# The second score product of the B heads, from a contraction of 64 rows to one of 128

## The chip, the cores and the metric

The kernel runs on one core of one Trainium2 chip. The metric is the device time of one execution in microseconds (us), smaller is better. TensorE is named PE in the profile (its weight loads PEld), VectorE DVE, ScalarE ACT, GpSimd POOL, SyncE SP.

## The reference, cut to what matters

The model is a decoder trunk of two layers on one sequence of 512 tokens with 1024 features. Each layer is an attention part and a gated MLP. The attention part has 16 heads in three groups that share one input and one output projection: A (4 heads, differential attention), B (6 heads, a mixture of dilated windows) and C (6 heads, a learned forget bias). The change touches B alone:

```python
qb = apply_rope(heads(qb, B_HEADS), cos_b, sin_b)          # 6 heads of 64 features
kb = apply_rope(heads(kb, B_HEADS), cos_b, sin_b)
ob = dilated_mixture_attention(qb, kb, heads(vb, B_HEADS))
# inside, for each of three dilated windows:
s = jnp.einsum('bgnqd,bgnkd->bgnqk', qb, kk).astype(jnp.float32) * (hd ** -0.5)
```

All of it is float32. The score of a query and a key is the product of two vectors of 64 features. The kernel forms the mixture of the three windows as one softmax with a mask that carries the logarithm of how many windows hold a pair, so that each B head needs one score matrix, causal, of 512 by 512.

## The kernel before, in words

**Splitting into high and low.** PE multiplies numbers of the type fp32r, which keeps fewer bits than float32. So each operand is split in two: the high part is what fp32r keeps (a copy on ACT), and the low part is the rest (a subtraction on DVE). A product then takes several matmuls: high by high, low by high, high by low. In the projections that is the helper `mm3` (lines 265 to 267), three matmuls of 512 columns for each tile of 128 features.

**Layout of q and k.** Heads are worked on in pairs; a pair fills 128 rows (partitions), 64 for each head, and `H0`, `H1` are the two halves. `stack_gen` (from line 427) builds the operands of a pair from the projection after rope. For q (`side == 0`) there is one tile for each head, with the high part in the head's own half and the low part in the other half. For k (`side == 1`) of the B heads there is one tile for each head with the high part in both halves (the first copy at line 436, the second at line 447), and a third tile, shared by both heads, with the low part of each head in its own half (line 433 is the subtraction). C heads have four tiles on each side; their second tiles hold 64 rows plus 4 rows of the forget bias.

**Score products.** `emit_S` (from line 620) makes the scores of one block: 128 queries against n keys, n being 128, 256, 384 or 512 for the four blocks of a head. Line 630 contracts all 128 rows: (high and low of q) by (high of k twice). For B heads line 632 then adds 64 rows: high of q by low of k, taken from the half `r` of the head. For C heads line 634 adds the 68 rows of their second tiles instead. A heads take one matmul of 96 rows (line 640).

**Order of the work.** In each layer eight pairs are worked on in the order B0 B1 A0 C0 A1 C1 B2 C2. Each pair has eight blocks (two heads of four). For a block come the scores (PE), the mask with its row maximum (line 653, DVE), the exponential (line 666, ACT), then two blocks later the transposes (line 694, PE), the split of the transposed weights (lines 713 on ACT and 718 on DVE) and the product with v (lines 740 and 741, PE). In between `fill` puts matmuls of the projections that later pairs need: the q and k chunks of the next pair (`qk_chunk`) and the v projections (`v_half`), and for the last pair the output projection. Post-processing (rope, `stack_gen`, the splits, the end of a head) stands in generators on a list; `tick` takes one step of each after every few matmuls. The tile framework orders each engine's instructions from this and sets the semaphores.

**Buffers.** All q and k operand tiles come from one pool of 14 tiles (`QKB`) of 128 by 512. A pair of B heads takes 5 of them, a pair of A or C heads 8.

**Around it.** While layer 0's attention runs, a stream of modulation weights is multiplied on POOL (line 221) and summed on ACT (line 224), for later use. The weights of the projections are loaded by DMA in order, and split on ACT (line 174) and DVE (line 186).

Of the kernel before, what the change touches and what calls it, by code (L numbers as in the profile page):

```python
# [8 lines left out]
F32 = mybir.dt.float32  # L9
F32R = mybir.dt.float32r  # L10
AF = mybir.ActivationFunctionType
# [19 lines left out]
def kernel(  # L31
# [27 lines left out]
    V, A, T, G = nc.vector, nc.scalar, nc.tensor, nc.gpsimd  # L59
# [15 lines left out]
    def tmp(name, tag):  # L75
        if tag == "rp":
            return rpp[0].tile([128, SEQ], F32, tag=tag, name=name, bufs=4)
        return tp.tile([128, SEQ], F32, tag=tag, name=name, bufs=4)
# [37 lines left out]
    for l in range(DEPTH):  # L116
# [16 lines left out]
        for m in range(KC):  # L133
            for b in range(0, FC, 8):
                n = min(8, FC - b)
# [117 lines left out]
    def split_gen(src, hi, lo):  # L253
        A.activation(out=hi, in_=src, func=AF.Copy)
        yield
        V.tensor_tensor(out=lo, in0=src, in1=hi.bitcast(F32), op=ALU.subtract)
        yield
# [23 lines left out]
    H0, H1 = slice(0, 64), slice(64, 128)  # L281
# [97 lines left out]
    def layer_attn(l, ap, mods, st, rt0):  # L379
        h = st.h  # L380
# [48 lines left out]
        def stack_gen(src, side, res, pair=None):  # L429
            R = (H0, H1)  # L430

            def sub(out, h):
                V.tensor_tensor(out=out, in0=src[R[h]], in1=res[h][R[h]].bitcast(F32), op=ALU.subtract)

            for h in range(2):
                A.activation(out=res[h][R[h]], in_=src[R[h]], func=AF.Copy)
                yield
                if side == 0:
                    sub(res[h][R[1 - h]], h)
                elif pair is None:  # L440
                    sub(res[2][R[h]], h)
                else:
                    sub(res[2 + h][H0], h)
                yield
                dup = res[h][R[1 - h]] if side == 1 else res[2 + h][H0] if pair is not None else None
                if dup is not None:
                    A.activation(out=dup, in_=src[R[h]], func=AF.Copy)
                yield
            if pair is not None:
                while not aug:  # L450
                    yield
                for h in range(2):
                    c = 24 * side + 4 * (2 * (pair - 5) + h)
                    nc.sync.dma_start(out=res[2 + h][64:68, :].bitcast(F32), in_=aug[0][c:c + 4, :].bitcast(F32))
                yield

        def qk_post(idx, side, ps, kind):
            n = 2 + side if kind == "B" else 4
            res = [ap.tile([128, SEQ], F32R, tag="qk", name="qk", bufs=QKB) for _ in range(n)]
            qks[idx, side] = res  # L460
            if kind == "C":
                yield from stack_gen(ps, side, res, ORDER[idx][1])
                qkdone.add((idx, side))
                return
            tb = rope_tile(kind)
            qf = tmp("qf", "rp")
            A.activation(out=qf, in_=ps, func=AF.Copy)  # L467
            sw = tmp("sw", "rp")
            nc.sync.dma_start(out=sw[0::2, :], in_=qf[1::2, :])
            nc.sync.dma_start(out=sw[1::2, :], in_=qf[0::2, :])  # L470
            for _ in range(5):
                yield
            V.tensor_tensor(out=qf, in0=qf, in1=tb[:, 0, :], op=ALU.mult)
            yield
            V.tensor_tensor(out=sw, in0=sw, in1=tb[:, 1, :], op=ALU.mult)
            yield
            V.tensor_tensor(out=qf, in0=qf, in1=sw, op=ALU.add)
            yield
            if kind != "A":
                yield from stack_gen(qf, side, res)  # L480
            else:
                hi, lo = sw.bitcast(F32R), qf.bitcast(F32R)
                yield from split_gen(qf, hi, lo)
                yield
                for m in range(4):
                    r = slice(32 * m, 32 * m + 32)
                    for j, t in enumerate((hi, lo, hi) if side == 0 else (hi, hi, lo)):
                        nc.sync.dma_start(out=res[m][32 * j:32 * j + 32, :].bitcast(F32), in_=t[r, :].bitcast(F32))
                    yield
            qkdone.add((idx, side))  # L490
# [3 lines left out]
        def rope_tile(kind):  # L494
            if kind not in rt:
                rt.clear()
                rt[kind] = load_rope(kind)
            return rt[kind]
# [6 lines left out]
        def qk_chunk(idx, side):  # L505
            ps = mm.tile([128, SEQ], F32, tag="mm", name="qkps")
            yield from feat_q(ps, W.use(), h)
            g = qk_post(idx, side, ps, ORDER[idx][0])
            next(g)
            aux.append(g)  # L510
# [111 lines left out]
        def emit_S(b):  # L622
            idx, kind, hh, i = blocks[b]
            q, k = qks[idx, 0], qks[idx, 1]
            n = 128 * (i + 1)
            qb = slice(128 * i, 128 * i + 128)
            if kind != "A":
                s = ps_s.tile([128, SEQ], F32, tag="s", name="s")
                r = (H0, H1)[hh]
                T.matmul(s[:, 0:n], q[hh][:, qb], k[hh][:, 0:n], start=True, stop=False)  # L630
                if kind == "B":
                    T.matmul(s[:, 0:n], q[hh][r, qb], k[2][r, 0:n], start=False, stop=True)  # L632
                else:
                    T.matmul(s[:, 0:n], q[2 + hh][0:68, qb], k[2 + hh][0:68, 0:n], start=False, stop=True)
                S[b] = [s]
                return
            res = []
            for mp in range(2):
                s = ps_s.tile([128, SEQ], F32, tag="s", name="s")
                T.matmul(s[:, 0:n], q[2 * hh + mp][0:96, qb], k[2 * hh + mp][0:96, 0:n], start=True, stop=True)  # L640
                res.append(s)
            S[b] = res
# [145 lines left out]
        for side in range(2):  # L788
            g = qk_post(0, side, st.qps[side], ORDER[0][0])
            next(g)  # L790
            aux.append(g)
# [14 lines left out]
        def ready(b):  # L806
# [5 lines left out]
            while not done(idx):  # L812
                tick()

        emit_S(0)
        lag = 2
        f1, f2, f3 = 0.06, 0.055, 0.055
        for b in range(nb + lag):
# [21 lines left out]
            if b + 1 < nb:  # L840
                ready(b + 1)
                emit_S(b + 1)
# [149 lines left out]
    with ExitStack():  # L992
# [7 lines left out]
        with tc.tile_pool(name="start", bufs=1) as stp:  # L1000
# [19 lines left out]
            for op in STARTUP:  # L1020
# [4 lines left out]
                else:  # L1025
                    k = int(op[1])
# [162 lines left out]
```

## Time and profile before

| what | value |
|---|---|
| time of three runs, median (lowest, highest) | 1345.78 us (1345.72, 1348.15) |
| span of the profiled execution, first to last instruction | 1343.3 us |
| median time less that span | 2.5 us |
| PE busy (share of the span) | 1289.3 us (96%) |
| DVE busy | 869.7 us (65%) |
| ACT busy | 663.8 us (49%) |
| POOL busy | 92.3 us (7%) |
| mean granted clock of PE, as a share of full speed | 0.991 |

The profile shows the execution from the first to the last instruction of the program; the profiled execution's own time stands there as this span alone, and what lies around it is taken as the difference to the median, 2.5 us. Busy times are sums over instructions; a matmul's duration in the records overlaps the next one's, so that PE is read best by the starts of successive matmuls. The attention part of layer 0 lies at about 64 to 300 us, that of layer 1 at about 719 to 945 us; the six stretches in which B heads are worked on are 64 to 93, 93 to 124, 234 to 257, 719 to 745, 745 to 776 and 881 to 903 us.

### The profile page before, as it was taken

What the parts mean: (1) busy time and instruction counts of PE and PEld (TensorE: products, weight loads), DVE (VectorE), ACT (ScalarE), POOL (GpSimd) and SP (SyncE); (2) the same over time, 40 slices, a digit from 0 to 9 for tenths busy, and PEclk for the clock granted to TensorE, in tenths of its full rate; (3) what the DMA queues carried; (4) which work ended last, traced back from release to release, by engine and by line L of the source; (5) the groups of instructions that cost most, each with busy time, mean ns of one, the idle gap of its engine ahead of it and who ended that gap; (6) DMA issues with size and microseconds to landing.
All of it is one profiled execution on the core that took longest, in us unless ns stands there. A gap on an engine that the chain in (4) does not pass through costs nothing.

```text
span 1343.3 us, 18226 instructions
## 1 busy us (share of the span) xinstructions
PE 1289.3 (96%) x6568; PEld 1058.5 (79%) x6568; DVE 869.7 (65%) x1733; ACT 663.8 (49%) x1242; POOL 92.3 (7%) x64
## 2 busy tenths in 40 slices
PE   3899898999999999999999999999999999999997
PEld 1678787688888888888898888878978888888886
DVE  7888989868888886422357687875754444443332
ACT  5567888954433333322345676775543333333231
POOL 5222423400000000000000000000000000000000
PEclk8899999999999999999999999999999999999999
DMA  9344453432777774233422234212123232222331
GB/s 374 142 142 150 162 155 130 133 116 85 252 250 257 249 252 139 91 98 99 130 83 94 85 105 123 79 59 83 54 94 94 95 96 97 100 91 91 101 100 63
DMA packets 68127, 174.44 MB, mean 130 GB/s; under 512 B 9410, under 2 KB 11730, under 8 KB 68036
## 3 DMA queue, kind: packets, MB, share of 16 engines
q1 hardware_dynamic: 66884, 172.16, 39.3%
q8 instruction: 52, 0.85, 0.3%
q10 hardware_dynamic: 1088, 1.05, 0.2%
q14 instruction: 39, 0.32, 0.1%
q0 software_dynamic: 64, 0.06, 0.0%
HBM read 159.41 MB, written 2.10 MB: 120 GB/s over the span
## 4 chain that ended last, share of the span: by engine, by line
PE 68%; DVE 5%; ACT 3%; issue 2%; DMA 1%; SPq 0%; DVEq 0%; ACTq 0%
PE pu L265 6%; PE pg L266 6%; PE pg L267 6%; PE pu L267 6%; PE pu L266 6%; PE pg L265 6%; PE dps L265 6%; PE dps L267 6%; PE dps L266 6%; PE qkps L265 2%; PE ops L266 2%; PE ops L265 2%; PE ops L267 2%; PE qkps L266 2%; PE qkps L267 2%
## 5 line engine op out<-in xcount | busy, mean ns | idle before, releaser
L186 DVE TENSOR_TENSOR wlo<-raww,whi 128x1024 fp32r<-128x1024 f32 (+3 forms) x188 | 229.5, 1221 | 238.2 <-ACT whi L174 234.2
L174 ACT ACTIVATE whi<-raww 128x1024 fp32r<-128x1024 f32 (+3 forms) x188 | 194.5, 1035 | 344.3 <-PE dps L266 138.0
L266 PE MATMUL pg<-hl,whi 128*128 128x512 f32 (+1 forms) x368 | 143.0, 389 | 0.4 <-DVE hl L314 0.2
L265 PE MATMUL pg<-hh,whi 128*128 128x512 f32 (+1 forms) x368 | 141.5, 385 | 1.6 <-ACT whi L174 1.6
L265 PE MATMUL pu<-hh,whi 128*128 128x512 f32 (+1 forms) x368 | 142.3, 387 | 0.0
L267 PE MATMUL pg<-hh,wlo 128*128 128x512 f32 (+1 forms) x368 | 140.9, 383 | 1.1 <-DVE wlo L186 1.1
L266 PE MATMUL pu<-hl,whi 128*128 128x512 f32 (+1 forms) x368 | 140.7, 382 | 0.0
L267 PE MATMUL pu<-hh,wlo 128*128 128x512 f32 (+1 forms) x368 | 140.6, 382 | 0.0
L265 PE MATMUL dps<-mh,whi 128*128 128x512 f32 x308 | 121.5, 395 | 0.0
L267 PE MATMUL dps<-mh,wlo 128*128 128x512 f32 x308 | 121.5, 394 | 0.0
L266 PE MATMUL dps<-ml,whi 128*128 128x512 f32 x308 | 121.2, 393 | 0.0
L666 ACT ACTIVATE e<-e,nm 128x256 f32<-128x256 f32 (+3 forms) x160 | 88.9, 556 | 32.4 <-DVE nm L653 30.5
L265 PE MATMUL qkps<-hh,whi 128*128 128x512 f32 x224 | 98.3, 439 | 0.6 <-ACT qf L467 0.2
L653 DVE CUSTOM_DVE_ANT_0 e<-s,cst 128x256 f32<-128x256 f32 (+3 forms) x160 | 76.8, 483 | 21.3 <-PE s L632 9.2
L906 ACT ACTIVATE y<-y 128x512 f32<-128x512 f32 x44 | 27.8, 632 | 126.3 <-DVE y L903 116.7
L266 PE MATMUL qkps<-hl,whi 128*128 128x512 f32 x224 | 89.5, 400 | 0.0
L267 PE MATMUL qkps<-hh,wlo 128*128 128x512 f32 x224 | 89.0, 397 | 0.0
L267 PEld LDWEIGHTS pu<-hh,wlo 128*128 128x128 f32 x368 | 69.1, 188 | 16.5 <-DVE wlo L186 1.1
L266 PEld LDWEIGHTS pg<-hl,whi 128*128 128x128 f32 x368 | 69.0, 188 | 16.6 <-DVE hl L314 2.0
L267 PEld LDWEIGHTS pg<-hh,wlo 128*128 128x128 f32 x368 | 69.0, 188 | 16.5 <-DVE wlo L186 1.9
L265 PEld LDWEIGHTS pg<-hh,whi 128*128 128x128 f32 x368 | 69.2, 188 | 16.0 <-ACT whi L174 2.0
L221 POOL TENSOR_TENSOR rawm<-rawm,scb 128x512 f32<-128x512 f32 x48 | 69.5, 1458 | 163.4 <-DMA rawm<-in_wmod_dram 119.5
(182 smaller groups left out, 2814.7 us busy)
## 6 DMA issues: line engine op xcount, KB each, us to landing
raww<-in_wup_dram SPq DMA_DIRECT2D x88, 512.0 KB
rawm<-in_wmod_dram SPq DMA_DIRECT2D x160, 256.0 KB
raww<-in_wqk_dram SPq DMA_DIRECT2D x32, 512.0 KB
raww<-in_wdown_dram SPq DMA_DIRECT2D x32, 512.0 KB
mu<-in_wmod_dram SPq DMA_DIRECT2D x16, 512.0 KB
raww<-in_wout_dram SPq DMA_DIRECT2D x16, 448.0 KB
raww<-in_wv_dram SPq DMA_DIRECT2D x12, 512.0 KB
raww<-in_wdown_dram SPq DMA_DIRECT2D x16, 384.0 KB
```

Source lines behind the costliest of these rows:

```text
L174: A.activation(out=h[:, 0:m], in_=self.raw[i][:, c:c + m], func=AF.Copy)
L186: V.tensor_tensor(out=lo[:, 0:m], in0=raw[:, c:c + m], in1=h[:, 0:m].bitcast(F32), op=ALU.subtract)
L221: G.tensor_tensor(out=raw, in0=raw, in1=scb[:, 512 * half:512 * half + 512], op=ALU.mult)
L265: T.matmul(ps[:, c], w[0], rhs[0][:, c], start=first, stop=False, skip_group_check=True)
L266: T.matmul(ps[:, c], w[0], rhs[1][:, c], start=False, stop=False, skip_group_check=True)
L267: T.matmul(ps[:, c], w[1], rhs[0][:, c], start=False, stop=last, skip_group_check=True)
L653: anchor[0] = V.tensor_tensor_reduce(out=e[:, 0:n], in0=s[:, 0:n], in1=cst[:, mask + SEQ - n:mask + SEQ], scale=-scale, scalar=3e38, op0=A ...
L666: anchor[1] = A.activation(out=e[:, 0:n], in_=e[:, 0:n], func=AF.Exp, bias=nm, scale=-1.0, accum_out=den).ins
L906: last_silu[0] = A.activation(out=y, in_=y, func=AF.Silu).ins
```

## The change

k of the B heads gets a tile of its own for the low part of each head, instead of one for both heads, so that a B pair takes 2 tiles for q and 4 for k. The low part is written into the head's own half as before (line 433) and then copied by ACT into the other half. The second matmul of a block contracts all 128 rows: (high and low of q) by (low of k twice). The score so takes up the product of the two low parts, which was left out before.

```diff
--- before.py
+++ after.py
@@ -438,13 +438,15 @@
                 if side == 0:
                     sub(res[h][R[1 - h]], h)
                 elif pair is None:
-                    sub(res[2][R[h]], h)
+                    sub(res[2 + h][R[h]], h)
                 else:
                     sub(res[2 + h][H0], h)
                 yield
                 dup = res[h][R[1 - h]] if side == 1 else res[2 + h][H0] if pair is not None else None
                 if dup is not None:
                     A.activation(out=dup, in_=src[R[h]], func=AF.Copy)
+                if side == 1 and pair is None:
+                    A.activation(out=res[2 + h][R[1 - h]], in_=res[2 + h][R[h]].bitcast(F32), func=AF.Copy)
                 yield
             if pair is not None:
                 while not aug:
@@ -455,7 +457,7 @@
                 yield
 
         def qk_post(idx, side, ps, kind):
-            n = 2 + side if kind == "B" else 4
+            n = 2 + 2 * side if kind == "B" else 4
             res = [ap.tile([128, SEQ], F32R, tag="qk", name="qk", bufs=QKB) for _ in range(n)]
             qks[idx, side] = res
             if kind == "C":
@@ -626,10 +628,9 @@
             qb = slice(128 * i, 128 * i + 128)
             if kind != "A":
                 s = ps_s.tile([128, SEQ], F32, tag="s", name="s")
-                r = (H0, H1)[hh]
                 T.matmul(s[:, 0:n], q[hh][:, qb], k[hh][:, 0:n], start=True, stop=False)
                 if kind == "B":
-                    T.matmul(s[:, 0:n], q[hh][r, qb], k[2][r, 0:n], start=False, stop=True)
+                    T.matmul(s[:, 0:n], q[hh][:, qb], k[2 + hh][:, 0:n], start=False, stop=True)
                 else:
                     T.matmul(s[:, 0:n], q[2 + hh][0:68, qb], k[2 + hh][0:68, 0:n], start=False, stop=True)
                 S[b] = [s]
```

## Rows read from the trace of the kernel before

**Rows 1.** Waits of PE, 64 to 124 us, then 719 to 776 us: total, times, longest

```profile
PE s L630 <- DVE nm L653: 0.2, 1, 0.2
...
PE qkps L265 <- ACT qf L467: 0.2, 1, 0.2
```

**Rows 2.** Chain of waits, 719 to 776 us, shares by line

```profile
by line: PE qkps L265 16.3%; PE qkps L266 13.3%; PE qkps L267 12.1%; PE s L632 9.5%; PE pt L694 8.8%; PE vps L417 6.6%; PE vps L418 6.6%; PE vps L419 6.6%; PE s L630 4.4%; PE po L740 3.7%; PE po L741 3.3%; PE pf L547 2.5%; PE pf L548 2.1%; 
```

**Rows 3.** Windows: length, busy by engine (instructions), granted clock, DMA share, GB/s

```profile
64.00:93.00 29.00, 28.84 (x166) 23.07 (x165) 25.67 (x60) 19.01 (x45) 9.59 (x7) 1.00 0.48 156
93.00:124.00 31.00, 30.85 (x182) 25.06 (x181) 25.89 (x68) 23.70 (x60) 5.53 (x4) 1.00 0.37 116
234.00:257.00 23.00, 21.95 (x108) 15.75 (x107) 19.67 (x46) 21.16 (x53) 8.43 (x7) 1.00 0.41 133
719.00:745.00 26.00, 26.00 (x149) 21.29 (x149) 21.09 (x60) 15.59 (x36) 0.00 (x0) 0.94 0.37 122
745.00:776.00 31.00, 30.85 (x179) 24.96 (x178) 21.30 (x50) 19.21 (x43) 0.00 (x0) 0.99 0.25 71
881.00:903.00 22.00, 21.30 (x107) 15.80 (x107) 14.91 (x35) 16.13 (x36) 0.00 (x0) 1.00 0.14 44
```

**Rows 4.** Timeline of PE, B block of 512 columns: start, duration, line, operands

```profile
73.81 0.40 PE L630 MATMUL s<-qk 128*128 128x512 f32 x1
74.14 0.50 PE L632 MATMUL s<-qk 64*128 64x512 f32 x1
74.56 0.50 PE L265 MATMUL qkps<-hh,whi 128*128 128x512 f32 x1
74.90 0.40 PE L266 MATMUL qkps<-hl,whi 128*128 128x512 f32 x1
```

**Rows 5.** Timeline of PE, C block of 512 columns

```profile
279.03 0.40 PE L630 MATMUL s<-qk 128*128 128x512 f32 x1
279.26 0.40 PE L634 MATMUL s<-qk 68*128 68x512 f32 x1
279.50 0.39 PE L265 MATMUL ops<-oh,whi 128*128 128x512 f32 x1
279.73 0.39 PE L266 MATMUL ops<-ol,whi 128*128 128x512 f32 x1
```

**Rows 6.** Timeline of PE, B block of 128 columns

```profile
77.66 0.22 PE L630 MATMUL s<-qk 128*128 128x128 f32 x1
77.81 0.32 PE L632 MATMUL s<-qk 64*128 64x128 f32 x1
78.07 0.50 PE L265 MATMUL qkps<-hh,whi 128*128 128x512 f32 x1
78.41 0.40 PE L266 MATMUL qkps<-hl,whi 128*128 128x512 f32 x1
```

**Rows 7.** Timeline of PE, C block of 128 columns

```profile
164.80 0.22 PE L630 MATMUL s<-qk 128*128 128x128 f32 x1
164.85 0.28 PE L634 MATMUL s<-qk 68*128 68x128 f32 x1
164.97 0.45 PE L265 MATMUL qkps<-hh,whi 128*128 128x512 f32 x1
165.25 0.40 PE L266 MATMUL qkps<-hl,whi 128*128 128x512 f32 x1
```

**Rows 8.** Timeline of PE's weight loads, second products of B, then C

```profile
74.13 0.18 PEld L632 LDWEIGHTS s<-qk 64*128 64x128 f32 x1 [0.36 <-issue]
...
279.03 0.19 PEld L634 LDWEIGHTS s<-qk 68*128 68x128 f32 x1
```

**Rows 9.** ACT's copies at line 447: times, min/median/max ns, first and last start

```profile
L447 ACT ACTIVATE qk<-qf x12: 614/630/632, 62.5 to 881.4; 64x512 fp32r<-64x512 f32 x12
```

**Rows 10.** Timeline of ACT before B2's first block in layer 0

```profile
234.32 0.62 ACT L447 ACTIVATE qk<-qf 64x512 fp32r<-64x512 f32 x1
234.97 0.62 ACT L666 ACTIVATE e<-e,nm 128x384 f32<-128x384 f32 x1
```

## Prediction

> **What bounds the kernel now.** I read the waits of PE first, then the chain of waits, the windows, and last the starts of single matmuls.
>
> In the first two B pairs PE has almost no idle time: its only wait is 0.2 us long in 60 us of layer 0, and 0.2 us in 57 us of layer 1 [rows 1]. The chain of waits through the same stretch of layer 1 consists of PE alone in its large entries, and 9.5% of it, 5.4 of 57 us, stands at line 632, the second score product of B, against 4.4% at line 630, which multiplies as many columns [rows 2]. So time taken from PE there should reach the end, as long as no other engine is just as late. The windows say who could be [rows 3]: DVE is busy 25.67 of 29 us in layer 0's B0 (89%), and ACT 21.16 of 23 us in layer 0's B2 (92%, the highest share in these six windows). In layer 1, where no modulation stream runs beside attention, DVE and ACT have 19% to 40% to spare. After attention nothing of the change is left, and a gain or loss is carried to the end.
>
> **What a 64-row product costs.** The reader should look at starts, not durations. A B block of 512 columns has starts at 73.81 (line 630), 74.14 (line 632), 74.56 and 74.90 (two projection matmuls): 1.09 us from the first to the last [rows 4]. The same four matmuls in a C block, with 68 rows in the second, start at 279.03, 279.26, 279.50 and 279.73: 0.70 us [rows 5]. All have 512 columns. The B block loses 0.10 us before the 64-row matmul, 0.18 us in it and 0.11 us in the matmul behind it: 0.39 us in all. With 128 columns it is 0.75 us [rows 6] against 0.45 us [rows 7], a loss of 0.30 us. The weight loads show how: the load for a C block's second product starts at 279.03, with the first product, and is over when it is needed; the load for a B block's starts at 74.13, just before its own matmul, after PEld has idled 0.36 us without waiting for another engine [rows 8]. The loads do not run ahead around a 64-row matmul. A 68-row product between two 128-row ones has none of this, and line 630 itself, with 128 rows, follows its neighbours without it, so I expect the 128-row second product to cost what the 68-row one does.
>
> **The change part by part.**
>
> *The matmul.* There are 3 pairs x 2 heads x 4 blocks x 2 layers = 48 blocks. At 0.30 us each PE is freed of 14.4 us, at 0.39 us of 18.7 us. Blocks of 256 and 384 columns lie between; I take the middle, 0.34 us, which is 16.3 us, or 2.7 us for each of the six pairs.
>
> *What of it reaches the end.* Layer 1: 3 x 2.7 = 8.1 us; DVE needs 21.09 of 26 us in B0, so it fits in 23.3 us. Layer 0's B1 gives its 2.7 us too: at the highest share seen, 0.92, its DVE work of 25.89 us fits in 28.1 of 31 us. Layer 0's B0 would need 25.67/0.92 = 27.9 of 29 us, so between 1.1 and 2.7 us; I take 1.9. Layer 0's B2 has ACT at 0.92 already, so between 0 and 2.7 us; I take 1.3. Together 8.1 + 2.7 + 1.9 + 1.3 = 14.0 us.
>
> *The copies.* ACT gets two more copies of 64x512 for each pair, 12 in all. The nearest row is the copy at line 447, 630 ns [rows 9], so 1.26 us a pair and 7.6 us in the kernel. Each waits for the low part from DVE, and behind it on ACT stand the next head's high part, the end of the old pair's head, and the exponential of its last blocks. In B2 of layer 0 these stand close: the copy at 234.32 us is followed by an exponential at 234.97 us [rows 10]. For B0 the copy stands between the rope and the first block's second product; projection matmuls cover it if the order places them there. The bounds are 0 (all covered by PE's other work) and 7.6 us (all on the path). As PE bounds these stretches and has fill work of its own, I stay nearer to the cover: 0.5 us for B0, 0.3 us for B1, and 0.35 us for B2, each in two layers, 2.3 us in all.
>
> *What costs nothing.* DVE makes as many subtractions as before. A B pair now takes 6 of the 14 operand tiles instead of 5; no pair's tiles are needed sooner by that, since the tile that a new one takes over is 14 allocations back, and for each pair that one belongs to heads that are done by then, or (the last two k tiles of C0, A1 and C1) to the same tiles as before. If I am wrong there, a pair's first block waits for the old pair's last score product. No DMA is added.
>
> *The sum.* 14.0 - 2.3 = 11.7 us less than a span of 1343.3 us, that is 1331.6 us. Around the span lie 2.5 us to the median of the runs shown, 1345.78 us; held fixed, the forecast is 1334.1 us.
>
> **Rules that speak against it.** The Trainium skill (TensorE: Matmul & The Clock Gate, section on loading the stationary operand) says that a load of few rows takes as long as one of 128, since only columns count; its section on packing small matmuls adds that a load overlaps a running matmul only when the two use different row groups. The loads here do last the same, 0.18 and 0.19 us, but the C block's overlaps a full-array matmul and the B block's does not, so the trace contradicts the second rule. By the first alone the change would free PE of nothing, by the second it would add exposed loads; both are rivals below, with times from rows.
>
> **The rivals.**
>
> - *All of it is kept (0.12).* ACT and DVE work that can wait moves aside, and the copies are covered: 16.3 to 18.7 us, so 1327.1 to 1329.5 us. A further 1.6 us would come if the half-clock stretch in layer 1's B0 went away (clock 0.94 over 26 us [rows 3]). For: PE never waits there. Against: 89% and 92% elsewhere.
> - *DVE and ACT take PE's place (0.12).* Layer 0 gives 1.1 us in B0 and nothing else, layer 1 gives 5.4 us in B0 and B1 and nothing in B2, and the copies cost 2.3 us: 4.2 us, 1341.6 us. For: the shares in layer 0. Against: 27% spare in layer 1's B2 (16.13 of 22 us on ACT).
> - *The number of rows does not matter (0.04).* Then the extra time lies in what stands beside the product, not in its rows, nothing is freed, and the copies alone stay: 1345.78 + 2.3 = 1348.1 us. Against: the 68-row rows.
> - *Slower by the copies (0.03).* They come at the start of each pair, where PE may run out of fill work. If both copies stall PE (1.26 us) long enough for its clock to halve (1.6 us more), a pair loses 2.9 us; six lose 17.2 us against 14.0, and the time is 1349.0 us. It decides from 2.3 us a pair on. For: the clock did halve once in layer 1's B0. Against: no wait of PE over 0.2 us there.
> - *Slower by exposed loads (0.01).* If a 128-row load cannot overlap a 128-row product, 48 loads of 0.19 us add 9.1 us, and with the copies the time is 1357.2 us.
>
> **How the numbers follow.** The likeliest case has 0.68 and lies at 1334.1 us, from 1330 to 1338 us as the kept part of layer 0 and the copies vary. I count less than 0.2%, 2.7 us, as no change, since runs of this kernel agree no better. Faster by more is 0.68 + 0.12 + 0.10 of the second rival = 0.90; within it are 0.02 of that rival and 0.03 of the third; slower gets the rest, 0.05. A range from 1328.0 to 1340.5 us holds the likeliest case, most of the first rival and some of the second, about 8 in 10.
>
> **What would show it.** In the profile after, the starts in a B block should lie as in a C block: 0.70 us over four matmuls of 512 columns, 0.45 us with 128. The share of line 632 in the chain through 57 us of layer 1 should fall from 9.5% to near line 630's. The windows of layer 1's B pairs should each be 2 to 3 us shorter, those of layer 0's B0 and B2 less, with DVE and ACT above 0.92 there if they take over. ACT should have 12 more copies of about 0.63 us; waits of PE for them at a pair's first block would be the price. The prediction is wrong if the gap in front of line 632 stays, if PE waits several us more for DVE or ACT in the B pairs, or if the later pairs give the time back.

## The result and the profile after

The changed kernel takes 1340.49 us (median of 6 runs, 1337.11 to 1344.54) against 1349.38 us for the kernel before in the same comparison (6 runs, 1345.72 to 1355.52). The ratio is 0.9933, with a 95% interval from 0.9906 to 0.9960: 9.0 us less, where 11.7 us were forecast. The three runs known beforehand were among the faster ones of the kernel before, so the ratio, and not the two medians, is set against the forecast: applied to their 1345.78 us it gives 1336.8 us, where 1334.1 us was forecast. The profiled run of the changed kernel took 1337.11 us at a span of 1335.3 us: 1.8 us lie around the span, not 2.5. Lines of the changed kernel lie up to two further down: its score products of B are lines 631 and 633.

**The matmul.** The starts of PE in a B block of the changed kernel, 512 columns and then 128 (start, duration, line, operands):

```profile
73.32 0.40 PE L631 MATMUL s<-qk 128*128 128x512 f32 x1
73.56 0.39 PE L633 MATMUL s<-qk 128*128 128x512 f32 x1
73.79 0.39 PE L265 MATMUL qkps<-hh,whi 128*128 128x512 f32 x1
74.02 0.39 PE L266 MATMUL qkps<-hl,whi 128*128 128x512 f32 x1
...
76.78 0.22 PE L631 MATMUL s<-qk 128*128 128x128 f32 x1
76.83 0.27 PE L633 MATMUL s<-qk 128*128 128x128 f32 x1
76.95 0.45 PE L265 MATMUL qkps<-hh,whi 128*128 128x512 f32 x1
77.23 0.39 PE L266 MATMUL qkps<-hl,whi 128*128 128x512 f32 x1
```

The four starts with 512 columns now take 0.70 us, against 1.09 us before [rows 4], and as long as C's [rows 5]. With 128 columns they take 0.45 us, against 0.75 [rows 6, 7]. The weight load of the second product starts with the first product and is over in time, where it had waited before [rows 8]:

```profile
73.33 0.19 PEld L633 LDWEIGHTS s<-qk 128*128 128x128 f32 x1
```

In the chain of waits through layer 1's first two B pairs (717.7 to 771.7 us in the changed kernel) line 633, the second product now, has 4.9%, where it had 9.5% [rows 2]; line 631 has 3.3%:

```profile
by line: PE qkps L265 12.9%; PE qkps L266 12.4%; PE qkps L267 12.1%; PE pt L695 9.1%; PE vps L419 7.0%; PE vps L418 7.0%; PE vps L417 7.0%; PE s L633 4.9%; PE po L741 3.7%; PE po L742 3.4%; PE s L631 3.3%; PE pf L549 2.5%; issue 2.4%; ACT q
```

**What became of it.** The six stretches with B pairs, from the first score product of the pair to that of the next pair (columns as in [rows 3]):

```profile
64.80:91.30 26.50, 25.83 (x164) 22.40 (x162) 23.49 (x57) 19.84 (x46) 10.51 (x6) 1.00 0.50 159
91.30:122.60 31.30, 29.24 (x182) 25.10 (x182) 27.28 (x70) 25.62 (x62) 5.88 (x6) 1.00 0.41 122
231.30:255.10 23.80, 21.38 (x115) 16.09 (x115) 19.56 (x47) 22.38 (x56) 8.77 (x7) 1.00 0.40 128
717.70:741.60 23.90, 23.57 (x151) 20.72 (x151) 21.37 (x58) 17.62 (x39) 0.00 (x0) 0.97 0.41 129
741.60:771.70 30.10, 29.90 (x184) 25.99 (x183) 21.50 (x51) 20.14 (x45) 0.00 (x0) 0.97 0.26 74
875.00:897.20 22.20, 21.13 (x116) 16.84 (x116) 16.78 (x36) 18.99 (x43) 0.00 (x0) 1.00 0.17 50
```

Layer 1's became 2.7, 1.7 and 1.6 us shorter (26.6 to 23.9, 31.8 to 30.1, 23.8 to 22.2 us, by the starts of the pairs' first products), 6.0 us together. The granted clock of the first two is 0.97: each trace has one half-clock stretch in this layer's attention, before inside B0 (from 742 us), after across the end of B0 (from 740 us), so that B0's gain is a little too large here and B1's too small. In layer 1's B2 PE now waits 1.5 us for DVE and ACT, where it had waited 1.0 us. Layer 0's B0 became 2.1 us shorter, B1 not at all (31.26 before, 31.31 after), B2 0.9 us. PE, which had one wait of 0.2 us there [rows 1], now has six in layer 0 (64 to 122.6 us), 2.7 us together:

```profile
PE s L633 <- ACT qk L449: 0.7, 1, 0.7
PE qkps L265 <- ACT qf L469: 0.6, 1, 0.6
PE po L741 <- DVE op L754: 0.4, 1, 0.4
PE pt L695 <- DVE ptl L719: 0.4, 1, 0.4
PE pt L695 <- DVE z L554: 0.3, 1, 0.3
PE s L631 <- DVE nm L654: 0.3, 1, 0.3
```

and two small ones in layer 1 (717.7 to 771.7 us):

```profile
PE pt L695 <- ACT e L667: 0.2, 1, 0.2
PE qkps L265 <- ACT qf L469: 0.2, 1, 0.2
```

**Where layer 0's B1 lost it.** The timeline of the changed kernel at the start of that pair, four of its rows on POOL, DVE, ACT and PE (idle time before an instruction and what ended it in brackets):

```profile
87.66 3.73 POOL L221 TENSOR_TENSOR rawm<-rawm,scb 128x512 f32<-128x512 f32 x2 [12.97 <-DMA rawm<-in_wmod_dram]
...
90.27 1.67 DVE L433 TENSOR_TENSOR qk<-qf,qk 64x512 fp32r<-64x512 f32 x1
...
91.97 0.63 ACT L449 ACTIVATE qk<-qk 64x512 fp32r<-64x512 f32 x1 [0.71 <-DVE qk L433]
...
92.65 0.33 PE L633 MATMUL s<-qk 128*128 128x128 f32 x1 [0.73 <-ACT qk L449]
```

The subtraction that makes the low part (line 433), 0.69 us in the median, takes 1.67 us and ends 0.55 us after POOL's two products. The new copy (line 449) waits 0.71 us for it, and the second product waits 0.73 us for the copy. The subtraction was late before too; then only the product needed it, and other work lay in front. The two rows of the kernel before:

```profile
88.26 3.58 POOL L221 TENSOR_TENSOR rawm<-rawm,scb 128x512 f32<-128x512 f32 x2 [12.87 <-DMA rawm<-in_wmod_dram]
...
91.38 1.00 DVE L433 TENSOR_TENSOR qk<-qf,qk 64x512 fp32r<-64x512 f32 x1
```

It ends 0.54 us after POOL's products there. Those start when their transfers are in, and end only 0.45 us sooner in the changed kernel (91.39 against 91.84 us), while PE starts the pair 1.75 us sooner. From PE's lead of 2.3 us at the end of B0 1.35 us are gone here; 1.5 us are won in the pair's blocks, and 0.75 us lost again at its end. The copy is not needed for such a loss: in the run without copies (below) PE waits 1.1 us for DVE at the same place (88 to 95 us).

**And in C2.** After B2, PE waits 1.5 us for the output of B2's head (line 256), which the output projection needs (0.7 us before), and its clock is granted at half for the next 3.4 us. First the wait of the changed kernel, 262 to 273 us, then two windows:

```profile
PE ops L266 <- DVE ol L256: 1.5, 1, 1.5
```

```profile
262.00:269.10 7.10, 5.57 (x29) 4.12 (x28) 5.96 (x11) 5.16 (x15) 4.90 (x4) 1.00 0.48 166
269.10:272.60 3.50, 3.50 (x13) 3.07 (x13) 2.66 (x6) 1.98 (x5) 0.58 (x1) 0.51 0.44 140
```

The lead at C2's first score product, 4.2 us against the first trace of before, is 1.4 us when the MLP starts. In a second trace of the changed kernel no half-clock stretch lies there, but two lie elsewhere in layer 0 (near 90 and 145 us), and its attention takes 264.8 us, where it takes 263.2 in the first. Their number differs from execution to execution: after the start the first trace of before has one (at 742 us), a second one five.

The copies are there, 12 of them, at the price forecast for one:

```profile
L449 ACT ACTIVATE qk<-qk x12: 611/628/631, 65.9 to 876.8; 64x512 fp32r<-64x512 f32 x12
```

### The profile page after: what moved, and what is told of

It is laid out like the page before. It is cut to its first block, busy times and chain, and to the rows that moved or that the text cites. A ratio compares the mean times of both kernels' runs of the same rounds, so it can differ in the third digit from the quotient of the medians.

```text
span 1335.3 us, 18235 instructions
## 1 busy us (share of the span) xinstructions
PE 1278.1 (96%) x6568; PEld 1058.2 (79%) x6568; DVE 868.8 (65%) x1733; ACT 671.5 (50%) x1254; POOL 94.1 (7%) x64
## 4 chain that ended last, share of the span: by engine, by line
PE 59%; DVE 9%; DMA 6%; ACT 4%; issue 2%; SPq 0%; DVEq 0%; ACTq 0%
PE dps L265 6%; PE dps L267 6%; PE dps L266 6%; DMA rawm<-in_wmod_dram 5%; PE pg L266 4%; PE pu L265 4%; PE pg L267 4%; PE pu L267 4%; PE pu L266 4%; PE pg L265 4%; DVE wlo L186 2%; PE ops L265 2%; PE ops L266 2%; PE ops L267 2%; DVE rawm L228 2%
```

## Experiments

Theory A: the copies on ACT, and the waits for them at a pair's start, ate layer 0's gain. Theory B: layer 0 is loaded by the modulation stream beside its attention, on ACT, DVE and POOL, so that a faster PE only waits there. Rival C: layer 0 loses to something else, as the ends of heads or half-clock stretches. Rival D came up last: the stream costs by itself, whatever PE does. All ratios are to the kernel before on the same chip, with 95% intervals.

**The changed kernel again.**

> The changed kernel itself, as the reference on this chip for the three variants beside it. Both theories: 8 to 9 us less than the kernel before (ratio 0.993 to 0.994). Layer 0 (up to the first gate product of its MLP) gives 1.5 to 2 of them, layer 1's attention 7.

0.9931 (0.9916 to 0.9946). The gain is the same; this is the reference for the next three.

**128 rows without copies.** Edit, on the kernel before:

```diff
-T.matmul(s[:, 0:n], q[hh][r, qb], k[2][r, 0:n], start=False, stop=True)
+T.matmul(s[:, 0:n], q[hh][:, qb], k[2][:, 0:n], start=False, stop=True)
```

> 128 rows without the copies: the kernel before, where the second product contracts all 128 rows of q's tile against the one shared low tile of k. It multiplies the low part of q by the low part of the other head's k, where the changed kernel has its own head's; no copies, no tile more. The matmul costs the same as in the changed kernel (four 512-column starts in 0.70 us). Theory A (the copies on ACT, and the waits for them at a pair's start, ate layer 0's gain): 12 to 15 us less than the kernel before, layer 0 giving 5 to 6. Theory B (layer 0 is loaded by the modulation stream on ACT, DVE and POOL, so that it can't use a faster PE): 8.5 to 11 us less, layer 0 still giving under 3.

0.9931 (0.9915 to 0.9948), the same as with the copies. Theory A falls: without any copy, layer 0's B1 is 30.7 us long, its attention takes 264.6 us (263.2 and 264.8 with the copies), and the whole gain is no larger.

**Copies without 128 rows.** Edit, on the changed kernel: the second product takes `q[hh][r, qb]` and `k[2 + hh][r, 0:n]` again.

> The copies without the 128 rows: the changed kernel, where the second product contracts 64 rows again, so that nobody reads the copied halves. Theory A: 4 to 7 us slower than the kernel before, most of it in layer 0. Theory B: 0 to 2 us slower; ACT busy 7.6 us more in both.

0.9990 (0.9977 to 1.0003). No cost of the copies can be seen; up to 0.4 us of slowdown and 3.1 us of gain are within the interval. Theory A missed again, and so did the forecast's 2.3 us. The one trace of this run is less plain: layer 0's attention takes 270.4 us, more than in either trace of the kernel before (265.0 and 267.1), and layer 1's 262.4 us, less (265.2 and 267.1). It has two half-clock stretches in layer 0 and none in layer 1, so the difference may lie in them; that the copies cost something in layer 0 alone is not ruled out.

**Copies by transfer.** Edit, on the changed kernel:

```diff
-A.activation(out=res[2 + h][R[1 - h]], in_=res[2 + h][R[h]].bitcast(F32), func=AF.Copy)
+nc.sync.dma_start(out=res[2 + h][R[1 - h]].bitcast(F32), in_=res[2 + h][R[h]].bitcast(F32))
```

> The changed kernel with the copies as transfers on SP's queue (as A heads' operands are moved) instead of on ACT. ACT is busy 7.6 us less than in the changed kernel; the first block of a pair waits for a transfer instead of a copy. Theory A, if it is ACT's time that costs: 11 to 14 us less than the kernel before; if it is the wait at a pair's start: as the changed kernel or worse, since a transfer takes longer than 0.63 us. Theory B: within 2 us of the changed kernel.

0.9920 (0.9902 to 0.9938), which the interval doesn't part from the changed kernel's 0.9931. It reaches into theory A's 11 to 14 us too, so it is the run without copies that decides, not this one.

**No stream in layer 0's attention, 64 rows and 128 rows.** Edit, on each kernel: `layer_attn` gets an empty list of stream units, and a memset fills the 24 columns of `modc` and the scale that comes from them.

> The kernel before without the modulation stream beside layer 0's attention (24 of its columns are set to a constant instead of computed; the rest is whole): no transfers, no products on POOL, no sums on ACT and DVE for them. It is the base for the next one. Both theories: faster than the kernel before, by 2 to 12 us, all of it in layer 0's attention.

> The changed kernel with the same left out. Theory B (the stream is what keeps layer 0 from using the faster PE): 13 to 15 us less than the kernel before without the stream, 6 to 7.5 from layer 0 and 7 from layer 1. Rival C (layer 0 loses its gain to something else: the pairs' starts, the end of B2's head before the output projection, half-clock stretches): still 8 to 10 us, layer 0 giving 2 to 3.

0.9908 (0.9888 to 0.9927) and 0.9804 (0.9784 to 0.9823); medians 1336.80 and 1323.28 us. Without the stream the 128 rows are worth 13.5 us by the medians, as theory B said, and rival C did not. The windows of layer 0's B0, B1 and B2 without the stream, with 64 rows:

```profile
65.20:95.00 29.80, 29.80 (x165) 24.02 (x163) 23.15 (x65) 18.26 (x41) 0.00 (x0) 0.94 0.42 133
95.00:126.30 31.30, 31.15 (x182) 25.22 (x181) 21.41 (x53) 18.53 (x44) 0.00 (x0) 1.00 0.27 77
228.80:252.70 23.90, 23.44 (x117) 17.08 (x117) 16.83 (x36) 17.96 (x41) 0.00 (x0) 1.00 0.16 48
```

and with 128 rows:

```profile
65.00:90.60 25.60, 25.60 (x165) 22.81 (x164) 21.54 (x57) 18.17 (x41) 0.00 (x0) 1.00 0.43 140
90.60:120.10 29.50, 28.96 (x183) 24.94 (x182) 22.62 (x61) 20.70 (x48) 0.00 (x0) 1.00 0.31 89
222.40:244.60 22.20, 21.15 (x117) 16.82 (x117) 16.76 (x36) 19.00 (x42) 0.00 (x0) 1.00 0.16 51
```

The three become 4.2, 1.8 and 1.6 us shorter (of B0's, 0.06 x 29.8 = 1.8 us are a half-clock stretch with 64 rows, granted clock 0.94), and the whole attention of layer 0 goes from 256.2 to 248.3 us.

**The stream without its sums on ACT, 64 rows and 128 rows.** Edit, on each kernel: in `mod_col` the ACT sum and the DVE addition behind POOL's product are left out, and the same memset fills the columns.

> The kernel before, where the stream's transfers and POOL's products stay, but the sums on ACT and the additions on DVE are left out (the same columns set to a constant). Base for the next one. If ACT's time is the load, about as fast as the kernel before without the stream; if POOL's products slow DVE, nearer to the kernel before.

> The changed kernel with the same left out. If theory B holds and ACT's sums are the load: 13 to 15 us less than the kernel before with the same left out. If theory B holds and it is POOL's products beside DVE: 8 to 11 us less.

1.0054 (1.0035 to 1.0073) and 0.9992 (0.9976 to 1.0008); medians 1356.92 and 1348.27 us. The base became slower by leaving work out, which neither side expected. Its timeline shows 11 of POOL's products between 63 and 92 us, where the kernel before has 6: with nothing to wait for behind them they come as fast as the transfers allow, and B0 takes 38 us. PE's longest wait there (64 to 104 us) is for DVE:

```profile
PE po L738 <- DVE ptl L715: 4.9, 1, 4.9
```

The 128 rows are worth 8.7 us here, as with the whole stream. So taking ACT's sums away does not set the gain free as long as POOL's products run; what is left is these products and their transfers. Since the products also came closer together, the pair does not show that ACT's sums cost nothing.

**The kernel before again, for a second trace.**

> The kernel before again, for a second trace of it. Within its runs, 1343 to 1354 us; layer 0's attention (from the first v projection to the first gate product) 265 to 270 us, where the first trace had 265.0, as the profiled run was one of the faster ones; layer 1's 265 to 268.

267.1 us in layer 0 and 267.1 us in layer 1. It also shows what the first trace had not: in layer 1's B2 the clock falls to half in the 64-row kernel, and the stretch takes 26.9 us instead of 23.8:

```profile
884.10:911.00 26.90, 26.51 (x116) 19.34 (x116) 16.75 (x36) 17.84 (x39) 0.00 (x0) 0.87 0.14 42
```

Three of the six traces with 64 rows have this, none of the eight with 128 rows: some of the gain in the medians may come from there, which so few traces do not show.

**64 rows in A's products.** Edit, on the changed kernel: `q[2 * hh + mp][0:64, qb]` and `k[2 * hh + mp][0:64, 0:n]` in line 641.

> The changed kernel, where the A heads' score products contract 64 of their 96 rows (the third of the three terms is left out), 64 products in all. If a 64-row product costs by its rows, each of them loses 0.30 to 0.39 us as B's did: 19 to 25 us of PE time, and 10 to 20 us on the end, as A's stages are not bound by PE alone. If the loss is in the change of mode between 64 and 128 rows, a 64-row product that directly follows another has no gap of 0.10 us before it, and the pairs of them that stand together lose about half as much each. If the loss belonged to something else in the B blocks (the half of the rows that starts at row 64, the shared tile), A's would lose nothing.

0.9989 (0.9968 to 1.0009), 1345.89 us against 1339.31 us for the changed kernel in its own comparison: the 64 products take 6 to 8 us on the end (the two comparisons ran on different chips; 7.8 us by the ratios), less than expected. Two of them that stand together, 512 columns each, in layer 1's A0 (the two are one row of this view, x2):

```profile
782.71 0.40 PE L267 MATMUL qkps<-hh,wlo 128*128 128x512 f32 x1
783.03 0.72 PE L641 MATMUL s<-qk 64*128 64x512 f32 x2
783.68 0.50 PE L265 MATMUL qkps<-hh,whi 128*128 128x512 f32 x1
784.02 0.39 PE L266 MATMUL qkps<-hl,whi 128*128 128x512 f32 x1
```

From 782.71 to 784.02 lie four steps of 512 columns, 1.31 us. At 0.70/3 us each [rows 5] they would take 0.93 us. The pair loses 0.38 us, as much as a single 64-row product [rows 4]. The place is typical: at that price by column, 19 of the 22 pairs in the trace lose 0.38 to 0.47 us, and most of the 20 products that stand alone 0.37 to 0.58 us. So it is the change between 64 and 128 rows that costs, not the number of rows. The Trainium skill (TensorEngine Tiling (Array Packing), Key Properties) says that a change of tiling mode drains the engine; this trace agrees, if a product of 64 rows is in a mode of its own, and gives the price, 0.3 to 0.4 us there and back.

**The stream on DVE, 128 rows and 64 rows.** Edit, on each kernel:

```diff
-return mod_col(l, ci, raws, l == 0 and 16 <= ci < 40)
+return mod_col(l, ci, raws)
-ms, mr = 4, 3.2
+ms, mr = 4, 1.6
```

> The changed kernel with the modulation stream of layer 0 as one multiply-and-sum on DVE for each half column, as it is done in the MLP part, instead of POOL's product and ACT's sum, and at half as many steps a block, since each half column has half as many. It computes the same. If it is POOL's products that slow DVE and ACT's sums that load ACT: 2 to 6 us less than the changed kernel (3 to 11 in all below the kernel before is what both would give; 11 to 15 tells it). If DVE's own time is the bound of layer 0, about 30 us more work on it makes it slower than the changed kernel by 2 to 10 us.

0.9895 (0.9877 to 0.9914), 1333.26 us (1331.42 to 1334.15): the fastest kernel here that computes all of it, about 5 us below the changed kernel and 14 us below the one before. DVE is busy for 213.29 us in layer 0's attention (64.8 to 310.6 us), hardly more than with the stream on POOL, while ACT is busy 29 us less than in the changed kernel:

```profile
64.80:310.60 245.80, 237.61 (x1404) 201.97 (x1403) 213.29 (x550) 166.94 (x367) 0.00 (x0) 0.98 0.46 141
```

> The kernel before (64 rows, shared low tile) with the stream on DVE as in the kernel that was 0.9895 of before. It says whether that kernel's extra 5 us are the 128 rows' gain in layer 0, set free, or the stream's own. Theory B (in layer 0 the faster PE was useless while POOL slowed DVE; with PE as slow as before, the stream's place hardly matters): 1343 to 1348 us, so that 128 rows are worth 11 to 14 us with the stream on DVE, as without a stream. Rival D (the stream on DVE saves its 5 us by itself, whatever PE does): 1340 to 1343 us, so that 128 rows are worth 7 to 9 us with it, as with the stream on POOL.

0.9993 (0.9978 to 1.0007), 1347.42 us. With 64 rows the stream on DVE gives nothing that can be measured. So the extra gain of the kernel above is the 128 rows' own, set free: by the ratios they are worth 13.2 us with the stream on DVE, 14.0 without a stream, 9.0 with it on POOL (by the medians 14.2, 13.5 and 8.9, the first across two chips). Each is good to 2 to 4 us by the intervals; it is that two different ways to free POOL agree, and the traces below, that set them apart from 9.0. Rival D falls. The stream's transfers go on in both runs with the stream on DVE, so they are not what held the gain.

| stretch, us by the starts in the traces | before, two traces | changed, two traces | no stream, 64 and 128 rows | stream on DVE, 64 and 128 rows |
|---|---|---|---|---|
| layer 0: B0 | 28.7, 29.8 | 26.6, 27.2 | 29.8, 25.6 | 28.2, 26.2 |
| layer 0: B1 | 31.3, 31.3 | 31.3, 30.4 | 31.3, 29.5 | 32.7, 31.2 |
| layer 0: B2 | 24.7, 24.5 | 23.8, 25.2 | 23.8, 22.2 | 22.2, 21.2 |
| layer 0: attention | 265.0, 267.1 | 263.2, 264.8 | 256.2, 248.3 | 262.9, 258.2 |
| layer 1: attention | 265.2, 267.1 | 258.2, 257.8 | 267.6, 258.0 | 267.7, 257.1 |
| half clock in layer 0's attention | 0, 6.8 | 3.4, 6.8 | 3.4, 0 | 6.8, 10.2 |
| half clock in layer 1's attention | 3.4, 10.2 | 3.4, 3.4 | 10.2, 3.4 | 10.2, 0 |

(Attention of layer 0 counts from its first v projection matmul, of layer 1 from the 25th matmul of its first q projection, 4.0 us after the first one, to the MLP's first gate product.)

The half-clock stretches blur the comparison of single traces. As an estimate from these rows, a stretch that PE works through at half clock loses half its length (layer 1's B2 above took 3.1 us longer with 6.8 us of it). Without that, the 128 rows shorten layer 1's attention by 5.5 to 7.0 us in all four pairs of traces, and layer 0's by 2.3 to 3.5 us with the stream on POOL, but by 6.2 us without a stream and 6.4 us with it on DVE.

## Why the prediction was right, and where not

The mechanism was right in the matmul and in layer 1, and 9.0 us less against 11.7 lies well inside the range; for layer 0 the account was wrong. By its steps:

- *A 128-row second product costs what a 68-row one does.* Right to the digit, 0.70 and 0.45 us. That the number of rows does not matter, and that 128-row loads cannot overlap, the third and the last rival, are out, and so are the first, in which all is kept, and the slower time by the copies. The cause behind the row is finer than I had it: not the 64 rows but the change to them and back.
- *Layer 1 gives 8.1 us, less 1.15 us for copies.* 7.0 us came, between the first traces, of it 6.0 us in the three B stretches, of which only B0 reached the 2 to 3 us forecast for each. The other pairs of the table show 9.3 to 10.6 us, where the 64-row trace has 10.2 us of half clock; the copies alone, with none, took 262.4 us, 4 to 5 us more than the changed kernel. So the part that is PE's work is nearer to 5.5 to 7.0 us, and that half clock can belong to the gain I had only as a bonus of 1.6 us in another rival.
- *Layer 0's B0 gives 1.9 us, less 0.5.* 2.1 us came (2.7 us between the second traces).
- *Layer 0's B1 gives its 2.7 us.* This is the step that failed: nothing came between the first traces, 0.9 us between the second. I took a stretch's mean share on DVE, 25.89 of 31 us, and the highest mean seen as what an engine can bear. But the stretch is not evenly loaded: at the pair's start DVE stood behind POOL, and the gain of the blocks was lost at both ends.
- *Layer 0's B2 gives 1.3 us, less 0.35.* 0.9 us came between the first traces, and between the second it was 0.6 us longer. And I had not looked behind it: in C2 the output projection waits for B2's head, whose end is on DVE and ACT, and the lead of 4.2 us was 1.4 us at the MLP. "A gain or loss is carried to the end" held for the MLP, not for the rest of layer 0's attention.
- *The copies cost 2.3 us.* Nothing that can be measured: copies alone 0.9990, no copies at all 0.9931, as with them. That the total came near is in part luck: the 2.3 us set aside for copies made up for part of what layer 0 did not give.

So the rival in which DVE and ACT take PE's place was half true, in layer 0 alone: 14.0 was put together from 6 us for layer 0 and 8 for layer 1, and it was 2 and 7. Two of the signs of being wrong came there: 2.7 us of waits of PE for DVE and ACT in B0 and B1, and C2 that gave time back. The reason for the difference between the layers is the stream: without it, layer 0's attention shortens by 7.9 us, with it on DVE by 4.7, with it on POOL by about 2 (6.2, 6.4 and 2.3 to 3.5 us without the half clock, as estimated above), and the times of whole runs say the same. That POOL's products are the part of it that matters rests on two pairs of runs, leaving ACT's sums out (no help) and moving the stream to DVE (help). The second also takes 29 us off ACT, so it does not part the two alone, and whether it is the waiting itself or its place in time stays open. DVE's sum of busy time does not tell it: in layer 0's attention of the 128-row kernels it is 183 us without the stream, 210 us with it on POOL and 213 us with it on DVE. So with the products on POOL the stream takes about as much of DVE's time as when DVE does all of it.

## What to carry to other kernels

Look at the starts of matmuls wherever a contraction of 64 rows stands between ones of more: here each such excursion cost PE 0.3 to 0.4 us or a little more, two in a row cost it once, and filling the other half of the rows cost nothing that could be measured. When PE is made faster, read the stretches between the waits of the next engine, not their mean share: a stretch with 84% on DVE gave nothing in one pair of traces and 0.9 of 2.7 us in another. And when a gain stays out in one of two like stages, run both kernels without what differs between the stages; here one pair of runs showed that the gain was there and that the stream held it; which part of the stream took two pairs more and is not settled to the last.

## What the runs showed of the hardware that was not expected

Instructions of DVE that read and write SBUF alone can wait out a product on POOL. An addition of one column (line 226) of the kernel before takes 0.15 us in the median and up to 1.26 us:

```profile
L226 DVE TENSOR_TENSOR mp<-mq,bm x24: 133/154/1114, 84.2 to 278.3; 128x1 f32<-128x1 f32 x24
L226 DVE TENSOR_TENSOR modc<-mq,mp x24: 132/156/1257, 88.3 to 280.3; 128x1 f32<-128x1 f32 x24
```

The 35 of these 48 that start beside no product take 0.16 us at most; the 13 that start beside one end within 0.1 us of its end, the 11 longest within 0.02 us. One of them, with its product:

```profile
240.50 1.98 POOL L221 TENSOR_TENSOR rawm<-rawm,scb 128x512 f32<-128x512 f32 x1 [0.26 <-ACT rawm L224]
...
241.25 1.25 DVE L226 TENSOR_TENSOR modc<-mq,mp 128x1 f32<-128x1 f32 x1
```

The three subtractions of line 433 that take longer than 0.69 us (1.00, 1.18 and 1.67 us) end 0.54 to 0.55 us after a product, but six others that start beside one are not lengthened. Line 718, which reads the transposed weights from PSUM, shows no such spread (0.54 to 0.69 us for its two sizes, also where it starts beside a product):

```profile
L718 DVE TENSOR_TENSOR ptl<-pt,pth x96: 536/558/693, 76.6 to 930.8; 128x384 fp32r<-128x384 f32 x64, 128x512 fp32r<-128x512 f32 x32
```

DVE is busy 30 us longer in layer 0's attention, where the stream runs, than in layer 1's (windows from the first score product to the first gate product), with 65 more instructions:

```profile
64.40:317.00 252.60, 240.46 (x1404) 198.23 (x1403) 211.08 (x502) 191.84 (x457) 68.60 (x49) 1.00 0.43 137
718.90:961.70 242.80, 238.56 (x1393) 198.11 (x1393) 181.38 (x437) 161.95 (x356) 0.00 (x0) 0.99 0.28 88
```

The Trainium skill (SBUF — State Buffer, section "SBUF: two separate sides") says that DVE and POOL share a pair of ports, which one instruction holds to its end against the other, for a DVE instruction with two inputs in SBUF among others; these rows agree with it. And leaving the sums of the stream out made the kernel slower, by 0.54%; the products, behind which nothing waited any more, came closer together, and PE's longest wait in the first pair was 4.9 us, for DVE.
